# The sums of the retention's block products on VectorE in place of GpSimd

## The chip, the cores and the metric

One core of a Trainium2 chip runs the whole program. The metric is the device time of one launch in microseconds (us); before the change the median of three runs is 1839.34 us, from 1838.33 to 1842.97. Five engines share the work: TensorE (PE), VectorE (DVE), ScalarE (ACT), GpSimd (POOL), and SyncE (SP), which issues loads.

## The reference

Two layers over 512 latent tokens with 256 context tokens in front, 1024 wide, in float32. The first layer is neighbourhood attention beside spatial gating, the second a two-way retention; each is followed by a gated feed-forward with a depthwise convolution. The part that the change touches is the input projection of the retention:

```python
    splits = [RET_QK_WIDTH, 2 * RET_QK_WIDTH, 2 * RET_QK_WIDTH + RET_V_WIDTH]
    q, k, v, g = jnp.split(h_lat @ w_in, splits, axis=-1)
    cos, sin = axial_rope(T, dk)
    q = apply_rope(q.reshape(B, T, H, dk), cos, sin)
    k = apply_rope(k.reshape(B, T, H, dk) * dk ** -0.5, cos, sin)
    ...
    for d in range(2):
        lg = log_decay[d].astype(jnp.float32)
        ...
        s_ctx = retention_final_state(rev(kc), rev(vc), lg)
        outs_lat.append(rev(retention_chunked(rev(q), rev(k), rev(v), lg, s_ctx)))
    y_lat = retention_output(outs_lat[0] + outs_lat[1], g, gn_g, w_out)
```

There are 8 heads; per head q and k are 128 wide, v and g 256.

## The kernel before

Every float32 matrix is split into a high part (ScalarE rounds it, line 225) and a low part (VectorE takes the rounded one from the whole, line 226), and each product is three matmuls of the parts (lines 269 to 272). `split` is the helper for this, and most rows on L225 and L226 in a profile are its two halves.

The retention goes head by head. Head 0 is computed plainly. From head 1 on the projections of a head onto the latent tokens are 2 by 2 block products that need seven block products instead of eight: q beside k (`qk_lat`) and v beside g (`vg_lat`) share them. For that, sums and differences of blocks are needed on both sides:

- of the tokens, once: `token_sums`, whose inner function `whole` (line 1275) puts the high and the low part of a token block together again, 8 times over 128x512;
- of the weights, in each of heads 1 to 7: `q_units` makes four sums of 128x512 in the raw tiles `rwk` and `rwq`, and `vg_units` four of 128x1024 in the raw tiles `rwv0`, `rwv1`, `rwg0`, `rwg1`, all through `less` (line 1293).

Each sum is then split: `rwq` are the split sums for q and k, `rwt` those for v and g. `blk` names token blocks, `w` weight blocks, and `xv`, `yv`, `zv` (`xk`, `yk`, `zk`) the products in PSUM. What else a head does: `rope` on q and k (ScalarE swaps halves into `swk` and `swq`, GpSimd multiplies them by the sine on line 1489, VectorE does the rest on lines 1488 and 1490); `decay` (the tables `e`, GpSimd on lines 1477 and 1478); scores `sd` of keys and queries; states `st` (VectorE on 1549); `across` (VectorE on 1612); `norm` (statistics and lines 1638 and 1646 on VectorE, the power on GpSimd, lines 1632 and 1635, into `rrr`), whose result `rg` is turned by TensorE (`rt`); and the output product `wr`, whose pieces ScalarE copies (`ypr`) and GpSimd adds to DRAM by DMA (`yd`, lines 1463 and 1465). Beside all this runs background work for the modulation of later sub-layers (`acc`, `ac`, `at`).

The order in which each engine takes its instructions is not that of the code. A packed table `ORDER` at the head of the file holds, engine by engine, the place of each instruction, and `queue` chains every engine's instructions in that order.

Of the kernel before, what the change touches and what calls it, by code (L numbers as in the profile page):

```python
# [18 lines left out]
P = 128  # L19
D = 1024  # L20
# [36 lines left out]
70M0x?I?CWMV-2`$;}u~a7)3ymZEOpZ3D<4cx3#Gw{!di1Rgwwmn;=a*ibH8R`>1Qx7G0+<K0d1P6*+CJ8Wm6--f$e5;FX*>RTFeU@NsosNjdz(t2x4Yi
O*s<p7jhra#D*0J_2b4xn?(9)|9%Qa79l19?<)Q!~^6W+z1nMgUT|Y&cYgh~}#_Krt8!_V=~RIOu30fJ__EjZaU(@DMdd<FE2&u`LB}Nuy5z?vw6@N9eA
<;t_Co2IjT_$cNE$>Hff`UIb}eym%R)k%5)vmAzhATNU>01*`7syGO?#0C<7*%HD|6(F#p~w+iH8(B0Jy9RR&O_`r{C{G`DFVRS^I_njS3EIoYV;TwaaH
_%LEr-8xou|61tKD@{<Kwtli-<*RU=)XEVG&~4n;{Zc#7x|3>Izgj5zRdvW7UjPb{)gb;P*mcH`Rfni5JU6jZWyo4diu`KVL#fhb_Z^rrF#K%7${!8(sd  # L60
Y$J$)Z$hwzel3Ru7%{~~*yDV-gs{ww=Bg=6pW<|c{*Xb0G9=#3X%Wus@#o;mx+_~qMdX8rfrK+^*QtLUcBWBdj_z#eZXhn`?Bu$yl%n0Er!sUpl?!iMG>
0WL2!;7vH27ab^~-3pMM1T^vZ*oBK1et}^m*frglT;_lSSD_cZs0+?&u0erZvc9dZt&Rr(7MHl?+>PGN=CU~crA9iM;=tY3O#kxA)2zP_-p5pkAB7Xg;W
m4cO;0@ra0BLM=VoDH{@PW5hi`1G(;2-lv%h73!=E3++gJqnHC8$H_ju1w2xuLEbE^lo@XyYXQt$Rbc!GU}LH>vAmUi||clyXe0JVeAbm8LFYqRiJ{fqN
|$IhQC<S)Xf84eMR<!h|Fas13F7(y$5knPmYkB!f-b`rpe^%!XvrIkk;YvfZHqO=VR4v@!Mr%s-_bIEMZ{W~>1H4XC%aPQzO=OCR4Ay&X5cfE#I+`C-wD
u(xa+1=p1a`_YNb+%Es`YHBFynn>WR}qO1ZXd)*!7eAC!kzYy+5ckD^?mm{_(%4?8IH|Y*nY@m*Wv5zO}6(R8G7pYkD2pZ?8Zp92J7Er_l(Z#3_iv3(Dr
QxzrijZdy37rJu(ZaR<zM?v!+k&9-4gUI*?~g!1QO>33@^=lFym5=Jwgw*|E;PY!5&7B*F$dFmh8%YYXJO@Cv)mk@CXDCt3JotmZa{t>MM9HlU#hX3$g0
# [35 lines left out]
gX1ORLAcU_s%o-Yf&a*Ui*a!JnH$Mn)ciQgs4$+x16$lC-BKi%B18~W`q*~e;!e4EcRIv%JWi5Sm8R(eK4}o;V=SV~IUob2?g&iW!WbF2e{l{E6tE?2nE
-UeD|Mr#$=-LiMYnV=%Os~NRbG8h<qK5YuUFwi!+SBLDX2Hy9mkHsiJKjrylhRBdhx=~vsW3xRZp|qd1bfzxScui8v8hVjfUF`;`iCVCi(hv49WTZR7?9
V6Nf|+r!}O~ud-(N5Sv(ij<puQ!>V^2?%%SeZ!q{a<At*u*VkbmVk*GG{PfiH)aiE^Oq_n3J<X_ExgWm4-exnfzvo>HfeYXl7*#N5k!63%{=yB!KSsRx4
1ZEiQLm;0&y#r+!Q;1D9&i65Lo1OoA(%tfrc!&OfyZDUhR>Zk=~i}*ew+=Fz{IGAI>7Ob+-Q;tCsb>{XQO%m?9Pku$r}PLj1l!tMYErDd(JI7H-cOJl@V
kp%CkAlTI#b9dnuk*+y`O^aNDm^Y-=F!!W^&e(k#HBYjZRjUTm{&MY1Ddc^zOfh#K7R>1lbWPDb@scxeo&Onj7obo)L+fl1rLUtlFF1WK41xpP8PTD<Qt
-94o$=<*tW4<BT_1WV8N5u_7$(sN)Q2rZY6M-J#N)5IpJ+`fu~abRol4Yo<QS9*{m_1lbB<DO+ZwL<=Y0I##mZHDlMNDk}Q^9B6ScAN2<KHolw-Uc)yh;
GnWo7scA$R=mW15U%e!LV^7<}Z_OZbtO1B?1IeJW*{Z_oCfLc))g>9Q61UmK#A!cqMdtOmRrj>{04ie5d$Vuc)Va4i3p}Drrt)AC%b;p{}2NEJ*k=>5z$
# [84 lines left out]
class Trunk:  # L193
# [1033 lines left out]
    def retention(self, y, final):  # L1227
        S, V, T, G, a = self.S, self.V, self.T, self.G, self.a
        KS = float(np.float32(P) ** np.float32(-0.5))
        with ExitStack() as ctx:  # L1230
# [31 lines left out]
            def token_sums():  # L1262
# [1055 lines left out]
```

## Time and profile before

| | us |
|---|---|
| median of three runs | 1839.34 |
| the profiled execution | 1838.39 |
| its span, first to last instruction | 1836.6 |
| TensorE busy | 1754.9 (96%) |
| VectorE busy | 1504.3 (82%) |
| ScalarE busy | 1108.7 (60%) |
| GpSimd busy | 517.6 (28%) |

Busy time is the time in which an engine has an instruction under way; an instruction that is held up while it runs counts as busy. Line numbers are those of the kernel before; in the changed one they are three higher from the table on, as the packed table is three lines longer there.

### The profile page before, as it was taken

How to read it: one execution, taken by the hardware profiler on the slowest of the kernel's cores; microseconds unless marked ns; L12 is line 12 of the kernel's file. 1: busy time of each engine (PE TensorE's matmuls, PEld its weight loads, DVE VectorE, ACT ScalarE, POOL GpSimd, SP SyncE). 2: the span in 40 equal slices, each digit the busy share in tenths (PEclk: the TensorE clock that was granted, in tenths of full speed). 3: DMA queues.
4: the chain of work that ended last, by engine and by line, in shares of the span. 5: the costliest groups of instructions: out<-in, count | busy, mean ns of one | idle time of the engine just before them, and what ended most of it. 6: DMA issues, size and time to landing. Idle time of an engine off the chain costs nothing. (4 is left out here: it accounts for less than half of the span.)

```text
span 1836.6 us, 29516 instructions
## 1 busy us (share of the span) xinstructions
PE 1754.9 (96%) x11108; PEld 1577.7 (86%) x11108; DVE 1504.3 (82%) x2430; ACT 1108.7 (60%) x2029; POOL 517.6 (28%) x574
## 2 busy tenths in 40 slices
PE   8999999999999999999989999889988989999998
PEld 4888888799999998998878888888877889999997
DVE  4887878898788878888898787876867799998887
ACT  7534668775556565556755555554544477676774
POOL 1102222311233222121354454444354110222221
PEclk9999999999999999999999999999998989999999
DMA  8445321454787777878514445444540344887773
GB/s 295 128 143 153 99 84 53 147 154 144 167 191 182 167 167 161 183 165 254 177 47 132 125 134 116 109 109 88 152 93 25 139 139 145 199 218 185 177 170 124
DMA packets 91380, 268.19 MB, mean 146 GB/s; under 512 B 11858, under 2 KB 12370, under 8 KB 91236
## 3 DMA queue, kind: packets, MB, share of 16 engines
q1 hardware_dynamic: 55620, 193.37, 32.7%
q0 software_dynamic: 33312, 64.54, 21.3%
q10 hardware_dynamic: 2304, 8.39, 1.2%
q8 instruction: 87, 1.43, 0.3%
q14 instruction: 57, 0.47, 0.1%
HBM read 193.89 MB, written 52.43 MB: 134 GB/s over the span
## 5 line engine op out<-in xcount | busy, mean ns | idle before, releaser
L380 DVE SCALAR_TENSOR_TENSOR acc<-ar,cs,acc 128x512 f32<-128x512 f32 x256 | 196.4, 787 | 10.2 <-DMA acc<-in_adab_row 4.1
L2006 POOL DMA_DIRECT2D yf<-yp x64 | 56.4, 973 | 260.2 <-ACT yp L2002 231.1
L269 PE MATMUL px<-hs,wc 128*128 128x384 f32 (+1 forms) x480 | 110.0, 309 | 0.2 <-ACT pre L1846 0.2
L269 PE MATMUL px<-blk,wb 128*128 128x384 f32 (+1 forms) x480 | 107.0, 308 | 0.0
L2002 ACT COPY yp<-wf 128x512 f32<-128x512 f32 x118 | 68.7, 584 | 60.5 <-PE wf L272 49.5
L1859 DVE SCALAR_TENSOR_TENSOR cv<-pre,cw,cv 128x769 f32<-128x769 f32 (+1 forms) x88 | 77.5, 884 | 28.9 <-ACT cv L1858 28.8
L1858 ACT ACTIVATE cv<-pre,cw 128x770 f32<-128x770 f32 (+1 forms) x88 | 81.0, 924 | 27.7 <-DVE pre L1851 19.7
L269 PEld LDWEIGHTS px<-hs,wc 128*128 128x128 f32 x480 | 81.3, 188 | 6.4 <-ACT pre L1846 1.0
L1846 ACT ACTIVATE pre<-px 128x256 f32<-128x256 f32 (+2 forms) x160 | 55.6, 369 | 50.7 <-PE px L269 32.7
L269 PEld LDWEIGHTS px<-blk,wb 128*128 128x128 f32 x480 | 80.1, 188 | 6.0 <-ACT pre L1846 1.3
L2006 POOL DMA_DIRECT2D yd<-yp x48 | 45.0, 954 | 142.1 <-ACT yp L2002 137.7
L2006 POOL DMA_DIRECT2D yd<-ypg x48 | 46.8, 1035 | 117.0 <-ACT ypg L2002 116.7
L1862 DVE SCALAR_TENSOR_TENSOR cv<-pre,cw,cv 128x769 f32<-128x769 f32 (+1 forms) x88 | 77.2, 883 | 1.0
L269 PE MATMUL px<-hs,wd 128*128 128x384 f32 x240 | 71.3, 337 | 0.0
L269 PE MATMUL py<-blk,wc 128*128 128x384 f32 x240 | 68.7, 337 | 0.0
L225 ACT ACTIVATE wb<-s 128x512 fp32r<-128x512 f32 x80 | 49.1, 628 | 31.6 <-PE px L269 29.0
L225 ACT ACTIVATE wc<-q 128x512 fp32r<-128x512 f32 x80 | 48.9, 625 | 22.3 <-PE py L269 11.0
L226 DVE TENSOR_TENSOR wb<-s,wb 128x512 fp32r<-128x512 f32 x80 | 54.3, 686 | 9.2 <-ACT wb L225 8.9
L226 DVE TENSOR_TENSOR wc<-q,wc 128x512 fp32r<-128x512 f32 x80 | 54.2, 687 | 4.2 <-ACT wc L225 3.9
L270 PE MATMUL wf<-fo,g 128*128 128x512 f32 x144 | 56.3, 397 | 0.4 <-ACT yp L2002 0.4
L271 PE MATMUL wf<-fo,g 128*128 128x512 f32 x144 | 56.4, 395 | 0.1
L272 PE MATMUL wf<-fo,g 128*128 128x512 f32 x144 | 55.5, 394 | 0.0
(1773 smaller groups left out, 7039.2 us busy)
## 6 DMA issues: line engine op xcount, KB each, us to landing
ar<-in_adaw SPq DMA_DIRECT2D x96, 512.0 KB
yf<-yp POOLq DMA_DIRECT2D x64, 256.0 KB, 5.0
yd<-yp POOLq DMA_DIRECT2D x54, 256.0 KB, 4.8
yd<-ypg POOLq DMA_DIRECT2D x54, 256.0 KB, 5.5
fin<-xd SPq DMA_DIRECT2D x8, 512.0 KB
xn<-in_x SPq DMA_DIRECT2D x6, 512.0 KB
xb<-in_x SPq DMA_DIRECT2D x6, 512.0 KB
xd<-xb ACTq DMA_DIRECT2D x6, 512.0 KB
```

Source lines behind the costliest of these rows:

```text
L225: self.S.activation(hi, src, AF.Copy)
L226: self.V.tensor_tensor(out=lo, in0=src, in1=hi.bitcast(F32), op=ALU.subtract)
L269: mm = lambda *p, **k: self.T.matmul(*p, skip_group_check=True, **k)
L270: mm(out, lhs[0], rhs[0], start=first, stop=False)
L271: mm(out, lhs[0], rhs[1], start=False, stop=False)
L380: V.scalar_tensor_tensor(out=acc[s], in0=raw[:, kk * 512 : kk * 512 + 512], scalar=self.cs[:, 8 * s + k : 8 * s + k + 1], in1=acc[s], op0= ...
L1846: S.activation(pre[:, i, c : c + w], ps[:, b : b + w], AF.Copy, scale=scale)
L1858: S.activation(d, s, AF.Identity, scale=w1, bias=b)
L1859: V.scalar_tensor_tensor(out=d[:, 1:W], in0=s[:, 0 : W - 1], scalar=w0, in1=d[:, 1:W], op0=ALU.mult, op1=ALU.add)
L1862: V.scalar_tensor_tensor(out=d[:, 0 : W - 1], in0=s[:, 1:W], scalar=w2, in1=d[:, 0 : W - 1], op0=ALU.mult, op1=ALU.add)
L2002: S.copy(v, ps)
L2006: G.dma_start((yd[t] if first else y[t])[:, o], v, accum_op=ALU.add)
```

## The change

Two helper functions issue to VectorE (`V`) what they issued to GpSimd (`G`), and the table of orders is another one. The number of instructions of the program is the same; 64 of them, 28 of 128x1024 and 36 of 128x512, change engines.

```diff
@@ ORDER
-c-oD82ecdKb>{sCGlRi241mF)_woR|-g_^6y^@cQkL9sS6sy=oijpWxlqI>yawJ){<w%x`Y{|AP+p*)mPP}olC7Wz=a*{YcC)rKBn@#MT-JDH1C!1{c-h
+c-oD82b3e%b>;h&P^bb5g#u8>IW^Ge1{$4n&S|Enr)PRXhY2Jn4~H|16T~4!QX)lCBu!DGC{lqGgJemhDA|&{mV<1cW39dR@p073I*#ijuhTl5vuk_zy^
...
@@ token_sums
                     def whole(x, n):
                         t = self.t2k(f"f{n}{m}", shape=(P, 2, 256))
-                        G.tensor_tensor(out=t, in0=x[0][:, c].bitcast(F32), in1=x[1][:, c].bitcast(F32), op=ALU.add)
+                        V.tensor_tensor(out=t, in0=x[0][:, c].bitcast(F32), in1=x[1][:, c].bitcast(F32), op=ALU.add)
                         return t
@@ retention
             def less(out, x, y):
-                G.tensor_tensor(out=out, in0=x, in1=y, op=ALU.subtract)
+                V.tensor_tensor(out=out, in0=x, in1=y, op=ALU.subtract)
```

On every engine the order is the same up to the end of the first feed-forward and again from the first blocks of the second one. Between them most instructions move by a few places on their engine. Three places follow. In the rows the trailing numbers are those of buffers, and the digit ahead of them is the head (`rwv05r` is the raw tile rwv0 of head 5).

GpSimd in head 5, around its first sums for v and g, before:

```order
L1293 TENSOR_TENSOR rwv05r_13110<-rwg05r_13112,rwv05r_13110 128x1024
L1477 TENSOR_TENSOR e05_12853<-e05_12853,e15_12855 128x384
L1478 TENSOR_TENSOR e05_12853<-e05_12853,ident_95 128x128
L1465 DMA yd1r_9102<-ypr_13032 128x512
L1489 TENSOR_TENSOR swk5_12973<-swk5_12973,sin_9095 128x512
L1465 DMA yd1r_9102<-ypr_13042 128x512
L1293 TENSOR_TENSOR rwg05r_13112<-rwg15r_13149,rwg05r_13112 128x1024
L1465 DMA yd2r_9103<-ypr_13052 128x512
L1489 TENSOR_TENSOR swq5_12983<-swq5_12983,sin_9095 128x512
```

VectorE at the same place, before:

```order
L226 TENSOR_TENSOR rwv15_13145<-rwv15r_13143,rwv15_13145 128x1024
L1380 TENSOR_TENSOR qs5_12876<-qs5_12876,yk5_12878 128x256
L226 TENSOR_TENSOR rwv05_13114<-rwv05r_13110,rwv05_13114 128x1024
L1488 SCALAR_TENSOR_TENSOR ks5_12875<-ks5_12875,cos_9093 128x512
L226 TENSOR_TENSOR rwt15_13178<-rwv05r_13110,rwt15_13178 128x1024
L1490 TENSOR_TENSOR ks5_12875<-ks5_12875,swk5_12973 128x512
L1488 SCALAR_TENSOR_TENSOR qs5_12876<-qs5_12876,cos_9093 128x512
L226 TENSOR_TENSOR rk15_12972<-ks5_12875,rk05_12971 128x512
L1490 TENSOR_TENSOR qs5_12876<-qs5_12876,swq5_12983 128x512
```

VectorE there, after the change:

```order
L229 TENSOR_TENSOR rwv15_13145<-rwv15r_13143,rwv15_13145 128x1024
L1383 TENSOR_TENSOR qs5_12876<-qs5_12876,yk5_12878 128x256
L229 TENSOR_TENSOR rwv05_13114<-rwv05r_13110,rwv05_13114 128x1024
L1296 TENSOR_TENSOR rwv05r_13110<-rwg05r_13112,rwv05r_13110 128x1024
L1491 SCALAR_TENSOR_TENSOR ks5_12875<-ks5_12875,cos_9093 128x512
L229 TENSOR_TENSOR rwt15_13178<-rwv05r_13110,rwt15_13178 128x1024
L1491 SCALAR_TENSOR_TENSOR qs5_12876<-qs5_12876,cos_9093 128x512
L1493 TENSOR_TENSOR ks5_12875<-ks5_12875,swk5_12973 128x512
L1296 TENSOR_TENSOR rwg05r_13112<-rwg15r_13149,rwg05r_13112 128x1024
L229 TENSOR_TENSOR rk15_12972<-ks5_12875,rk05_12971 128x512
L1526 SCALAR_TENSOR_TENSOR kd15_13086<-kn51_13095,e05_12853,kd05_13085 128x256
L1493 TENSOR_TENSOR qs5_12876<-qs5_12876,swq5_12983 128x512
```

The two sums of `rwv05r` and `rwg05r` stand on VectorE now, the first right behind the split that reads the same tile, the second ahead of the split of k; `rwt15`, the split of the first sum, has one VectorE instruction between itself and the sum, in which ScalarE makes the high part. The two adds of line 1490 (1493 now) still follow GpSimd's products.

GpSimd in the norm of head 6, before:

```order
L1632 TENSOR_SCALAR rrr6_14285<-rmv6_14284 128x2
L1635 TENSOR_TENSOR rrr6_14285<-rrr6_14285,mhalf_107 128x2
L372 DMA acc1100_16118<-in_adab_row 1x16x32
L1293 TENSOR_TENSOR rwv07r_14501<-rwg07r_14503,rwv07r_14501 128x1024
L1477 TENSOR_TENSOR e07_14336<-e07_14336,e17_14338 128x384
L1478 TENSOR_TENSOR e07_14336<-e07_14336,ident_95 128x128
L1293 TENSOR_TENSOR rwg07r_14503<-rwg17r_14540,rwg07r_14503 128x1024
```

GpSimd there, after:

```order
L1635 TENSOR_SCALAR rrr6_14285<-rmv6_14284 128x2
L1638 TENSOR_TENSOR rrr6_14285<-rrr6_14285,mhalf_107 128x2
L1480 TENSOR_TENSOR e07_14336<-e07_14336,e17_14338 128x384
L1481 TENSOR_TENSOR e07_14336<-e07_14336,ident_95 128x128
L375 DMA acc1100_16118<-in_adab_row 1x16x32
L1492 TENSOR_TENSOR swk7_14456<-swk7_14456,sin_9095 128x512
L1492 TENSOR_TENSOR swq7_14466<-swq7_14466,sin_9095 128x512
```

VectorE there, after:

```order
L1641 TENSOR_SCALAR on61_14305<-of6_14204,rmv6_14284,rrr6_14285 128x256
L1632 BN_AGGR rmv6_14284<-rbs63_14295 128x2
L1649 TENSOR_TENSOR rg6_13579<-on61_14305,rg6_13579 128x256
L1641 TENSOR_SCALAR on62_14308<-of6_14204,rmv6_14284,rrr6_14285 128x256
L1641 TENSOR_SCALAR on63_14311<-of6_14204,rmv6_14284,rrr6_14285 128x256
L434 SCALAR_TENSOR_TENSOR ab11_112<-at19_14474,ng_99 128x4
L1649 TENSOR_TENSOR rg6_13579<-on62_14308,rg6_13579 128x256
L1649 TENSOR_TENSOR rg6_13579<-on63_14311,rg6_13579 128x256
L229 TENSOR_TENSOR rwq37_14333<-rwk7r_14199,rwq37_14333 128x512
L1296 TENSOR_TENSOR rwg07r_14503<-rwg17r_14540,rwg07r_14503 128x1024
L1375 TENSOR_TENSOR ks7_14358<-ks7_14358,zk7_14362 128x256
```

Before, two sums and the two steps of `decay` stand on GpSimd right behind the power that `on` waits for. Now the two steps of `decay` alone follow it, and on VectorE the sum of `rwg07r` stands behind the last of the four products `rg`.

VectorE at the end of head 1, around the first sums for q and k of head 2, after:

```order
L1526 SCALAR_TENSOR_TENSOR kd11_10117<-kn11_10126,e11_9873,kd01_10116 128x256
L229 TENSOR_TENSOR rv11_9850<-vs1_10172,rv01_9849 128x512
L1445 TENSOR_TENSOR rg1_9851<-rg1_9851,xv1_10138 128x512
L383 SCALAR_TENSOR_TENSOR acc150_10019<-ar153_10475,cs_93,acc150_10019 128x512
L1592 TENSOR_TENSOR sd11_10343<-rs11_10342,e01_9871 128x256
L1296 TENSOR_TENSOR rwk2r_10479<-rwq2r_10597,rwk2r_10479 128x512
L1592 TENSOR_TENSOR sd11_10343<-rs11_10342,e01_9871 128x256
L1296 TENSOR_TENSOR rwq2r_10597<-rwq2r_10597 128x512
L229 TENSOR_TENSOR rwq12_10601<-rwq2r_10597,rwq12_10601 128x512
```

The first of these sums (`rwk2r`, with the loaded tile `rwq2r`) stands behind the add on `rg1` and a step of `acc`, and half of the scores `sd11` behind it. On SP's queue the loads of the retention exchange places by one to six; the load of `rwq1r` is among those that move back.

More of the change, by code (lines that the diff above doesn't have):

```diff
@@ L57 @@
[L57 to L66, printed above, removed]
@@ L102 @@
[L102 to L106, printed above, removed]
@@ new lines @@
+Y~;8(a0zX2qM6A(+KQ=<^W9z-A>D@+#0#vucd+-PxRbR+|L$Q0(Y6L`SMQWKmT!xK<A2NT#BOhKus1W+tsQ?bDon28NSA3zos7Zy*BjsWCy(`YaJX9w+I
+2?|C0bQn7yr%v6o#?2Usa!bM9)||_Y!v;`55EcB1!#Q#kyyv&^k@;L68%n1N+TPW@`|BTLyt{GU2_ewy5BO8i>xWyf7$o_qc3ufcgI_H-Llgc|&978jtG
+<zH>pB!#C!b}D0G-hI44{3#e-JwN=R4tK0LY_SDlJe3m>HL37y^i=QvqKAg1WP*2sz7V_4c$WIO%91fMgA5;FA+DI6#fj{A;{fY)i!<>GYeI`()#VSGXG
+fidVqlDVRL~Kt7C~OXCAS^}?cgao}TsW(Jm*mRB9HdzY|x70ex9zj1Zs1i*8wTX6*KdKD^wLk03M=<Mi(IzV?9e&Me*ep7#+FgzsF`}R8I@(<kq!2SKh_
+oJD}PJR8OBR$X$J@}A8fS%qdk1-2f(0g%kV6Y!XMgazD=lDPYouIifzbydh7KOhT{!XxQDw-nEx%=+LDTbB{oiJLS5qr+eVn5n0c6uK?MPmVU7|30?r{g
@@ new lines @@
+f>x_Umr4&fs+6tI9j{sw!7sqOXSf5E;<;n;nor9yE4Z2+roSM%9d*zn0yCr|wee)wfJweowcuX3Vq7rN;)7{A`9*|lQ9_b_{oJ@`6<IooR<&%w;y*w9=v
+z=g#k4#HkLXG0F{mW9+fpovFE&YnB_9>YlRmtF4hB@Q@n5xUWfI^dMvFes2q?!0#G-Zkn4SXktiYrN>)Oge@0pKqqCDGnO1-G*mr`7zep15YvyB3p3u2t
+2~Bv&o4o0QbY}%<K%z&t19*@WB0hR_KoI7umnCf9A)_IE)2=Uu8|(|B7RNSU~FloZhv*AAf9a<hu_XgooL?3^ISfuIi_5cBh9d1W-N*m9ytAUYda`J0G0
++pX|)(Y~~z%f#DR<Tz-aiHjkb>4g+ZAXW3@?%*g26u66=AX(vY7BzgIAbD4Y!LzG^9{e9%I=J8|4Z$2`WZv32>oS1~UdANOYmeP<&`VcE%fxBL@if5O0x
+{BfbQFbeM@44_<_8Qxhz4&?dIUGOY<SU582M-*?NWm`09>tUXKV$!kLB}sPK7;?w{+;36yvz1MI<*4dWN)(7|IN@-NB@l3zs2q!>eON7=h<zu^BRNCvkc
@@ new lines @@
+U}&EPlKx$Q^UOzoi=h*!}@zs)M2zj0~o-ur+&YYZmeU`OeIZX}<Rr;G!qUSr$sJ*h5!?J<N6bYSGB)@m!H9q=i3A4kfw=dQEB%dFgJ4qL;Ar~H71BA7u>
+DGcn);Qsa7UFp`l82?`7y(TiGdx~_*R>Lq*4A$c@=(Zsx$IvFf!G4ns-@M)5z!mU!;<vwMUt@d!8b2q9o`zILBT)Yt_OlG_0iiJbBKtD)@P|If9^za|NY
+nm-&V=r`6H$)_eAq_(L!4SU3R~MSW$%NZ^zu^}3=;L?rB*Y)Lm__0gBn1jao6(5T^XNM-i_#JnB_%-BV1+>>`Z7ca!D$Lz3Iz_Lj*w4G|1A)QxPeha)1Q
+oBy{eIb9x|V$+T1~pAQa>jgRFJc8fNmt=8EDY9^~gIcs>(NfQBoS`+XYc`bxQW#6EJY^H&z{*Kuj<E<g=V8;N)tyY8}vTfVW$odZvTXJHBS^z@S8MH()k
+!ydJeV9-3M^P@2Su<PJ*2fvK>&hOuy1j*P2HOw9#uXkbs3QmhIv-{y{ek(piS{~vHA3|?eZTY^gEV>heJ`*l*cqb1mr;qJlfQ)Rg#MKMiZK6g44xH!jGo
@@ new lines @@
+&K9n@y$kMW8O7(Zt4DdA<|t9W7UFWF1N@r2n1vG}*yw^+G0{(B65hs6(##^J!h9AYmr4k3AwYb~<DOkdm6>_4;9XNb6vw7!Zi<b&_B?d`3N&7<X{8@|Kd
+LyhEKT84$TfIsjV_6|!_788|0!}9|BDK<2$LDTfY%4gXGvc+|F1)S>rk1*9a(Afdq7h8Os>N-2ZAxQL-l<1-XL?hAq@3JR_H`%YVLx<sj+jV$p`BByk$B
+q|@TJpCk=%N32*!P&GBP<`->j+=iLb?b6cWHQ=eT*f|iC#AZ)_h3bW-sa?NCkChU09r+nghhJjYk+rU1Pg<T>;zlMhN8l%cvlH=pil({+0b3%k=mCF8+X
+UD3u->9!d|w(*oSN8=Y<Gp8gT|KF$m|Fgl12?fzZ%3vB;A7mmHozQFEWPC>wrAB5-TedLv-Xa=W>`lD=n&~7ajX6;}i*%c1qmuG0WvJ1w?`awm!2y1aug
+JhvtD7r$_31nH6ga63ji$d!^vp;5V@yzfL#kJYu?rGslYpdVe{QK-zIb<0>&EQ18r)6%w?1HXR4;+Mv(o^g>p+;~3HeO{jvsTmKz@e8J3JJ9Kb+)f%wbT
@@ new lines @@
+MD4X^HWA#<Td!zf4I&uwgO0M3?6@NR4xOIu%K2i&l(9MCZ~blA7CfXXk^RLVo=+LNrlmYbiucD2;>Fk7pwV>87<rt4=JJjV9U<%=tOUP6CJ<Rw5CfHCA0
+ly^(e>z+U~!3W}linh^7>ZPlvx3}!dwABEunQ@W2GD$+AYC!R@8)<{$j4N1(td5cnD>s)>Emh%7_7>9;P}>9}0<DKXhmXXLX0lyib6vEYO4qy?Rd-{jQ3
+Tl&htW>4_Il5{iK;A{t4-q*B9QAA>XRnaN=-=mD4$4#eTwawEu>%x2^prQr;2cXabZ7&<!`cvG9av|bdYOJ>YApsj$1wBI87bnFS1WCKWgX8Ut}RebwW$
+sF@!2Sk&2Q!w}Vq>a-QHxWc`3mDa=&0r4ogSUKcci(OsL*;SiALVXdEFGtv%Re4@2?-IMa-(@{x-zhfR|TH>HeT(9_GqB9yvfSD|HWHa4XCX1NsP<nc8^
+ygS-%u#EOfo{8zvtwGR$s#EqbSCh_-kwQKgL0hcga|v4gtdLoqJJ$l#3*T8_!j#%Q{Khk&xX`&2-7sfGqVM+GS8u<SDB=x{V;LZWum3CV^9rF^!s!9>kM
@@ new lines @@
+{xVjL>=)^-{yr6waCb|k=6f(r*-F6f>?{LSTkD6LUC8nJjROy1oNH9z%y*1jpQQ{Dap2NTeXp9(8*;A<=-C7URKuYQFkjH{nyb4P8(K%jn`U5NlH(Kpx^
++0@4KtnR9|E}<W9W&<HP<*E+!m(itAiEmtqMS33`*JHkZpwuqx291az+=CN<vzQ#f$seE;<=Aly8><ssJV6P9ziSb^h@KDz#PGp^c`y~O?mb2>->T=;Ts
+3g^V8EY<M$%1lz0kEUexbMLQpSd^OBXMtRyH$z{Rnp})jX_?VwTXnMjW?J;w_PE<g~5TE{GHd8bqvjL>svSz}6n{rqTvjWbZtfc)ECKYBL?Q69^~ciTcz
+-l#@zw8CrzX7zoHCv!(OfwyV3TWOz<bPi<!g2HoMZ1A4ZRm}mO?=1mn%h7t->mU^DXLCFn73Q$r`!lgnQg^#Wk+{m=wVLyj~5Q`hGfdjwAX8KSL?>@BK^
+2k;e-EsfCfg!m9v%MtV(T~GJX-5sv+sez&vFF)BYWe*0%)ftG*A{44`GIg=jkIa{M86WT`!lFmkWI81Os*&u3I`}F+R1u)59wO5Fg2)aoo9=Ir9dZUT)F
@@ new lines @@
+yPBnIrCP-o$cL`kwL$~csrR0dszN*MA^g+oIgK@H=h^?gb6f<TD?{~SG$%08L{$&CMX{*97|B>E9Mkt5v#ZC#<fk4_?c1x><9qCC2kPTEv83^zol=D{fy
+KDd86{()b4ha6lOfDi3YqtXotc1|=_dNF~NWYgW)F3F2GYU2VgiYnkUK|)60%EssCPoyFPcu==fz|dO52e)C~-UX^gA)qy=m=rNd>f4nxrHs;!hPpYAG*
+*Qe4fqDkTT&ZsuaAs!El#FDX(Q17co+TW2&D0$e~9-_7ZiuA!OnZkDX^!4-spIvd10pt<xp;|#nYeY^FKP!8uLzi$w~Lz=$OzjdgD#wm&UR--2CO%LH9K
+-#Rr%>Wv_T5uDVrIO-IDI(1bybqL6l~Ad99YOF^FWfG)ad4tQZtabsMY(9l1qD;#RWt~hJj&FY!NDVCU-dP0e|(3pDKF@u&<9Ar%1C6Y!epYB^0xZPa*#
+-H%nZ3R4XZJZzMCBXjySL-VQ
```

205 lines of the change are left out of this document (94 added, 111 removed).

## The prediction

> **What bounds the kernel now.** First I read the busy time by stretch of the span. The columns are the stretch and its length in us, then the busy us (and instructions) of TensorE (PE), its weight loads (PEld), VectorE (DVE), ScalarE (ACT) and GpSimd (POOL), the granted TensorE clock, the DMA share and GB/s.
>
> ```profile
> 0.00:800.00 800.00, 790.08 (x4479) 689.37 (x4480) 644.36 (x1134) 490.26 (x953) 186.23 (x264) 1.00 0.60 154
> 930.00:1480.00 550.00, 489.47 (x3430) 450.69 (x3428) 431.11 (x635) 292.24 (x479) 230.71 (x190) 0.96 0.42 112
> 1480.00:1600.00 120.00, 118.70 (x856) 111.53 (x856) 114.58 (x182) 88.01 (x163) 14.82 (x17) 0.97 0.55 153
> ```
>
> TensorE is the bound, and outside the retention there is little to win: it is idle for 10 of the first 800 us and for 1.3 of the 120 behind it. The retention, 930 to 1480, is the exception: 60.5 us idle (550 less 489.47) and a clock of 0.96, which is another 22 us (0.04 times 550). The instructions that the change moves, and nearly all that it puts in another order, are there too. Next I asked what TensorE waits for in that stretch: the waiting instruction, what released it, us in total, times, the longest.
>
> ```profile
> PE rt L1659 <- DVE rg L1646: 6.7, 4, 4.7
> PE xv L269 <- DVE rwt L226: 5.9, 4, 1.9
> PE yv L271 <- DVE rwt L226: 5.8, 3, 3.9
> PE rx L270 <- ACT st L225: 5.7, 5, 2.1
> PE zk L270 <- DVE of L1612: 3.8, 1, 3.8
> PE ac L418 <- ACT ah L225: 3.6, 1, 3.6
> PE pf L270 <- ACT hb L225: 3.4, 1, 3.4
> PE rs L272 <- DVE rk L226: 3.3, 1, 3.3
> PE ac L418 <- DVE al L226: 2.7, 1, 2.7
> PE kn L1519 <- DVE ks L1490: 2.6, 1, 2.6
> PE rs L270 <- ACT rq L225: 2.5, 1, 2.5
> PE rs L271 <- DVE rq L226: 1.5, 1, 1.5
> ```
>
> Mostly it waits for VectorE, which is busy for only 431 of the 550 us. So VectorE is late without being full. The timeline around the 3.9 us wait shows how (start, duration, instruction): first GpSimd, then VectorE, then TensorE.
>
> ```profile
> 1261.85 1.61 POOL L1489 TENSOR_TENSOR swk<-swk,sin 128x512 f32<-128x512 f32 x1
> 1263.69 2.99 POOL L1293 TENSOR_TENSOR rwg05r<-rwg15r,rwg05r 128x1024 f32<-128x1024 f32 x1
> ...
> 1261.94 5.83 DVE L226 TENSOR_TENSOR rwt<-rwv05r,rwt 128x1024 fp32r<-128x1024 f32 x1 [0.65 <-ACT rwt L225]
> ...
> 1267.83 0.39 PE L271 MATMUL yv<-rwt,s1r 128*128 128x256 f32 x1 [3.93 <-DVE rwt L226]
> ```
>
> One VectorE instruction took 5.83 us, and it ended 1.1 us after the second of two GpSimd instructions that had run since it began. The same shape elsewhere takes 1.22 us, as the rows for the feed-forward below show. So the two engines exclude each other while both read two tensors of SBUF, and the sums of lines 1275 and 1293 are most of what GpSimd does with tensors here.
>
> **The change, part by part.** Rows: GpSimd's time on lines 1293 and 1275; VectorE's free durations, in the second feed-forward (wa, 128x1024, and wc, 128x512); then the groups that are stretched in the retention.
>
> ```profile
> 930.00:1480.00 550.00, 118.88 (x56) 0.96 0.42 112
> 930.00:1480.00 550.00, 12.18 (x8) 0.96 0.42 112
> ...
> 1500.00:1740.00 240.00, 19.53 (x16) 1.00 0.70 176
> L226 DVE TENSOR_TENSOR wc<-q,wc 128x512 fp32r<-128x512 f32 x40 | 27.3, 687 | 2.1 <-ACT wc L225 2.1
> ...
> 930.00:1480.00 550.00, 55.77 (x28) 0.96 0.42 112
> L226 DVE TENSOR_TENSOR sd<-sd,sd 128x512 fp32r<-128x512 f32 x16 | 18.9, 1178 | 0.2 <-ACT sd L225 0.2
> L1490 DVE TENSOR_TENSOR qs<-qs,swq 128x512 f32<-128x512 f32 x7 | 9.8, 1394 | 5.5 <-POOL swq L1489 5.3
> L1490 DVE TENSOR_TENSOR ks<-ks,swk 128x512 f32<-128x512 f32 x7 | 9.2, 1313 | 2.7 <-POOL swk L1489 2.7
> L1488 DVE SCALAR_TENSOR_TENSOR qs<-qs,cos 128x512 f32<-128x512 f32 x7 | 9.2, 1310 | 0.9 <-ACT swq L1483 0.9
> L1488 DVE SCALAR_TENSOR_TENSOR ks<-ks,cos 128x512 f32<-128x512 f32 x7 | 5.1, 725 | 9.2 <-ACT swk L1483 9.2
> L226 DVE TENSOR_TENSOR rk<-ks,rk 128x512 fp32r<-128x512 f32 x7 | 7.8, 1114 | 4.9 <-ACT rk L225 4.8
> L226 DVE TENSOR_TENSOR rq<-qs,rq 128x512 fp32r<-128x512 f32 x7 | 7.4, 1056 | 0.0
> ```
>
> Off GpSimd: 64 instructions, 118.9 + 12.2 = 131 us. By itself this is worth nothing, as GpSimd is busy for 231 of 550 us. The transfers that GpSimd issues (the yd pieces) stay on its queue, behind fewer instructions. On SP's queue loads change places by one to six; in the stretch only two waits of a sum for a load show, those of the second rival below, and with them I price this.
>
> Onto VectorE: 28 sums of 128x1024 at 19.53/16 = 1.22 us are 34.2 us; 28 and 8 of 128x512 at 0.687 us are 24.7 us. Together 58.9 us.
>
> Back to VectorE: the time for which GpSimd held it up. The 28 rwt instructions (55.77 us) would take 34.2 free, so 21.6. sd: 16 times (1178 less 687) is 7.9. rk 3.0 and rq 2.6. The two groups of L1490: 7 times 707 and 7 times 626 ns, 9.3. L1488 on qs, against the 725 ns of the same instruction on ks: 7 times 585, 4.1. That makes 48 us. The last 13 (L1490, L1488) stand beside the products swk and swq, which stay on GpSimd, so between 35 and 48 come back; I take the middle, 42.
>
> So VectorE does about 17 us more in the stretch, 448 in place of 431. Is that on the path? In 1480 to 1600 it is busy for 114.58 of 120 us with TensorE at 118.70, so a share of 0.95 holds nothing up there; 448 us in some 510 is 0.88. The cover is VectorE's idle time, 119 us now. I charge the 17 us at the rate at which its work now makes TensorE wait (the rows above name VectorE for 32 us, over 431 busy), 1.3, and call it 2. If that cover is gone, the cost is the whole 17, or 24 with the lower figure.
>
> What TensorE gets: the waits whose releaser is one of the stretched groups or hangs on one: 6.7 (its rg stood behind locked instructions), 5.9, 5.8, 3.3, 2.7, 2.6, 2.5, 1.5, together 31.0 us. Not all of that is the moved sums' doing (swk has 1.6 of the 4.6 us in the timeline); against it I leave out zk and the ac behind ScalarE, 3.8 and 3.6 us, which come out of the same queues. I count no gain for the waits on st, which no stretched row explains. The new order of all engines inside the retention I cost at nothing of its own: it shifts most instructions by a few places, it is what has to place 64 new VectorE instructions where nobody waits, and no row prices that; its bounds are the rivals below.
>
> The clock follows the idle time. TensorE is idle in 1264 to 1268 and gets half its clock right afterwards:
>
> ```profile
> 1264.00:1268.00 4.00, 0.17 (x1) 0.17 (x2) 4.00 (x2) 0.00 (x0) 2.69 (x2) 1.00 0.71 96
> 1269.00:1272.00 3.00, 3.00 (x14) 2.71 (x12) 0.69 (x1) 0.63 (x2) 0.37 (x1) 0.50 0.00 0
> ```
>
> With 31.0 of 60.5 us of idling gone I take the same share of the 22 us: 11.3. [...]
>
> Sum: 31.0 + 11.3 - 2 = 40 us. The profiled execution took 1838.39 us (1836.6 of span and 1.8 around it), so 1798; the median of the three runs stands 0.95 above it, so 1799. The ends: nothing gained and VectorE's 24 us all on the path, 1863; all idling and the whole clock loss gone, 82 us, 1757. I stand nearer the middle because the waits that I count have rows of stretched instructions ahead of them.
>
> **The rivals.** First, a wash: VectorE only swaps time under the exclusion for work of its own. For it speaks that at several of TensorE's waits VectorE has been busy throughout, and that 58.9 us come for 35 to 48. What would be left is the shorter way through a sum: half of the 11.7 us of waits on rwt, 5.9, less 2: 1835. Against it: the 5.83 and 4.7 us are single stalls that work in pieces of 1.2 us doesn't make. [...]
>
> Second, slower: VectorE's queue stalls on a load. The first sum of each head's query and key weights needs loaded tiles, and in two heads GpSimd has waited for a load ahead of it:
>
> ```profile
> POOL rwk2r L1293 <- DMA rwq2r<-in_ret_qk: 8.3, 1, 8.3
> POOL rwk3r L1293 <- DMA rwo20r<-in_ret_out: 7.3, 1, 7.3
> ```
>
> On GpSimd nobody stood behind it; on VectorE the splits of scores and values do, and TensorE behind them. Two heads at these prices take 15.6 us of my 40. It decides from six heads on: seven times 7.8 is 55, less 40 is 15 slower, 1854. Against it: in five of the seven heads no such wait shows, and the new order puts the sum of head 2 behind the instruction that VectorE was at when the load had landed.
>
> Third, larger: with no 3 to 6 us stalls the new order closes most of the other waits as well, 55 to 82 us, about 1772. For it: the rest of the program runs with TensorE idle for 1%. Against it: st, hb and the handing over from head to head have no row that ties them to GpSimd.
>
> **How the numbers follow.** Forecast, 15 to 55 us faster, 1784 to 1824: 0.63. Wash, 1824 to 1844: 0.13. Slower: 0.11. Larger: 0.13. A measurement of this kernel can tell about 0.3%, 5.5 us. Faster than that are the forecast, the larger gain and half of the wash, 0.82; within it 0.07; slower 0.11. The range 1772 to 1834 leaves out half of the larger case and nearly all that lies above: about 0.2.
>
> **What would show it.** In the profile after: the sums on VectorE at 1.22 and 0.69 us; rwt near 34 us for 28 (38 with what swk and e still hold); GpSimd at about 95 us in the stretch; VectorE still about 448; no TensorE wait on rwt, rg or rk over 2 us; TensorE idle for about 30 us and the clock at 0.98. The prediction is wrong if waits of VectorE on loads appear ahead of the new sums, if sums stand right before instructions that TensorE waits for, or if swk, swq and e stretch VectorE as much as all of GpSimd does now.

## The result and the profile after

The changed kernel takes 1781.37 us (median of 4 runs, 1779.55 to 1782.02), the kernel before 1838.9 us in the runs beside it: 57.5 us less, a ratio of 0.9681 (95% interval 0.9664 to 0.9698). The profiled execution took 1781.4 us, with a span of 1779.6.

The whole difference lies in the retention. It ends 57 us earlier, so the stretch that answers to 930 to 1480 is 930 to 1423. The table by stretch (columns as in the prediction), with a window of the whole span for each kernel, the changed one first:

```profile
930.00:1423.00 493.00, 472.32 (x3414) 439.00 (x3412) 417.47 (x695) 291.37 (x475) 102.41 (x126) 0.99 0.46 120
1423.00:1783.00 360.00, 345.16 (x2416) 320.54 (x2416) 318.83 (x499) 242.57 (x441) 69.65 (x82) 0.98 0.63 166
0.00:1840.00 1840.00, 1736.87 (x11108) 1568.10 (x11108) 1492.42 (x2494) 1110.48 (x2029) 386.08 (x510) 0.99 0.55 146
```

```profile
0.00:1840.00 1840.00, 1754.93 (x11108) 1577.67 (x11108) 1504.33 (x2430) 1108.71 (x2029) 517.63 (x574) 0.99 0.55 146
```

TensorE is idle for 20.7 us of the stretch (493 less 472.32), before 60.5: 39.8 us. Its busy time falls by 17.2 us (489.47 to 472.32). Together these are the 57. Of the 17.2 us the clock explains 15.1: by the records of the granted clock, which the rounded 0.96 and 0.99 only approximate, half clock costs 5.1 us in this stretch, before 20.2. The surprise is in the VectorE column: 64 more instructions, and less time, 1492.42 us over the program in place of 1504.33.

What TensorE still waits for between 930 and 1423 (waiting instruction, releaser, us in total, times, longest):

```profile
PE rt L1662 <- DVE rg L1649: 4.3, 4, 2.1
PE rx L273 <- ACT st L228: 3.4, 3, 1.6
PE pf L273 <- ACT hb L228: 3.0, 1, 3.0
PE ac L421 <- ACT ah L228: 2.5, 1, 2.5
PE yk L274 <- DVE s1r L229: 1.7, 1, 1.7
PE kn L1522 <- DVE ks L1493: 0.8, 1, 0.8
```

The waits on `rwt`, `rk`, `rq` and `al` are gone. The same stretch for the tile `rwt` alone (busy us of TensorE, its weight loads, VectorE and ScalarE), and then two sums of the changed kernel, a wide and a narrow one, from the views of a tile and of a line (minimum, median and maximum in ns, first and last start):

```profile
930.00:1423.00 493.00, 112.56 (x672) 95.91 (x672) 33.93 (x28) 29.58 (x28) 0.99 0.46 120
```

```profile
L1296 DVE TENSOR_TENSOR rwv05r<-rwg05r,rwv05r x1: 1224/1224/1224, 1228.5 to 1228.5; 128x1024 f32<-128x1024 f32 x1
L1296 DVE TENSOR_TENSOR rwq1r<-rwq1r x1: 685/685/685, 933.4 to 933.4; 128x512 f32<-128x512 f32 x1
```

`rwt` takes 33.93 us where it took 55.77, so 1.21 us for each of the 28, its free time. Nothing holds it up any more.

### The profile page after: what moved, and what is told of

Its sections match the earlier page's. It is cut to its first block, busy times and chain, and to the rows that moved or that the text cites. A ratio compares the mean times of both kernels' runs of the same rounds, so it can differ in the third digit from the quotient of the medians.

```text
span 1779.6 us, 29484 instructions
## 1 busy us (share of the span) xinstructions
PE 1736.9 (98%) x11108; PEld 1568.1 (88%) x11108; DVE 1492.4 (84%) x2494; ACT 1110.5 (62%) x2029; POOL 386.1 (22%) x510
## 3 DMA queue, kind: packets, MB, share of 16 engines
q0 software_dynamic: 33312, 64.54, 21.9%
## 4 chain that ended last, share of the span: by engine, by line
PE 84%; DVE 6%; ACT 4%; issue 3%; POOL 2%; DMA 1%; SPq 0%; POOLq 0%; DVEq 0%; ACTq 0%
PE px L272 12%; PE wf L273 5%; PE wf L274 5%; PE wf L275 5%; PE xv L272 4%; PE py L272 4%; PE px L274 2%; PE px L273 2%; PE px L275 2%; PE yv L272 2%; PE xk L272 2%; PE py L273 1%; PE py L274 1%; PE py L275 1%; PE ug L274 1%
## 5 line engine op out<-in xcount | busy, mean ns | idle before, releaser
L383 DVE SCALAR_TENSOR_TENSOR acc<-ar,cs,acc 128x512 f32<-128x512 f32 x256 | 189.7, 760 | 7.2 <-issue 2.6
L1861 ACT ACTIVATE cv<-pre,cw 128x770 f32<-128x770 f32 (+1 forms) x88 | 81.1, 925 | 27.8 <-DVE pre L1854 20.0
L273 PE MATMUL wf<-fo,g 128*128 128x512 f32 x144 | 56.2, 397 | 0.1
L1635 POOL TENSOR_SCALAR rrr<-rmv 128x2 f32<-128x2 f32 x16 | 5.7, 358 | 232.0 <-DVE rmv L1632 232.0
L275 PE MATMUL wf<-fo,g 128*128 128x512 f32 x144 | 56.0, 394 | 0.0
```

The lines of the kernel that those rows point to most:

```text
L273: mm(out, lhs[0], rhs[0], start=first, stop=False)
L275: mm(out, lhs[1], rhs[0], start=False, stop=last)
L383: V.scalar_tensor_tensor(out=acc[s], in0=raw[:, kk * 512 : kk * 512 + 512], scalar=self.cs[:, 8 * s + k : 8 * s + k + 1], in1=acc[s], op0= ...
L1861: S.activation(d, s, AF.Identity, scale=w1, bias=b)
```

## The experiments

Three theories were open. *Exclusion*: the time came back because GpSimd no longer holds VectorE up. *Order*: it came from the refitted orders. *Short path*: a sum takes 1.2 in place of 2.7 us, and TensorE feels only that.

The table sums up all runs. "Against before" is the median less that of the kernel before in the same comparison (1836.45 to 1839.67 us in these), and in this form the changed kernel stands at -57.5. "Stretched" is worked out from the trace: for each VectorE instruction that starts in 930 to 1480, its time above the fast end (the 5th percentile) of its operation and shape in the same trace, where that is over 60 ns, summed. "Half clock" is what TensorE's stretches at half clock cost over the whole span, the last of them counted to its end. GpSimd's busy time is that of 930 to 1480.

| kernel | us | against before | ratio, 95% interval | stretched us | GpSimd us | half clock us |
|---|---|---|---|---|---|---|
| before | 1838.9 | 0 | 1 | 77.2 | 230.7 | 27.1 |
| changed | 1781.37 | -57.5 | 0.9664 to 0.9698 | 13.1 | 107.7 | 11.8 |
| move alone | 1804.08 | -35.6 | 0.9791 to 0.9824 | 14.6 | 116.2 | 14.5 |
| order alone | 1828.16 | -11.5 | 0.9926 to 0.9955 | 63.7 | 225.9 | 27.8 |
| changed, idle products | 1834.38 | -5.3 | 0.9960 to 0.9993 | 63.4 | 234.4 | 28.7 |
| changed, idle memsets | 1789.04 | -50.6 | 0.9713 to 0.9742 | 11.0 | 215.2 | 15.0 |
| changed, idle copies | 1841.73 | +4.9 | 1.0015 to 1.0034 | 54.4 | 320.4 | 27.7 |
| changed, narrow sums on GpSimd | 1788.16 | -48.7 | 0.9717 to 0.9746 | 30.3 | 157.1 | 9.9 |
| changed, wide sums on GpSimd | 1818.92 | -17.5 | 0.9889 to 0.9920 | 45.2 | 173.1 | 20.9 |
| changed, 92 products on VectorE | 1819.54 | -17.3 | 0.9889 to 0.9918 | 18.5 | 108.0 | 20.2 |
| changed, 28 products on VectorE | 1788.22 | -48.2 | 0.9724 to 0.9750 | 16.7 | 109.7 | 12.1 |
| changed, rope products moved too | 1779.64 | -57.2 | 0.9673 to 0.9706 | 6.8 | 88.4 | 9.8 |
| changed, norm's product on ScalarE | 1783.64 | -52.8 | 0.9697 to 0.9724 | 12.0 | 108.4 | 11.6 |
| changed, old order of loads | 1791.42 | -45.9 | 0.9738 to 0.9770 | 13.5 | 108.9 | 16.6 |

**The move and the order, each alone.** The first kernel has the two lines of the change and the old table, with the 64 sums put into VectorE's row; the second has the lines as before and the new table, with the sums put into GpSimd's row.

```diff
@@ move alone, against the kernel before
-                G.tensor_tensor(out=out, in0=x, in1=y, op=ALU.subtract)
+                V.tensor_tensor(out=out, in0=x, in1=y, op=ALU.subtract)
...
@@ order alone, against the changed kernel
-                V.tensor_tensor(out=out, in0=x, in1=y, op=ALU.subtract)
+                G.tensor_tensor(out=out, in0=x, in1=y, op=ALU.subtract)
```

> The 64 sums run on VectorE, and every other instruction of all engines keeps the order it had before; each sum stands in VectorE's queue where it started on GpSimd in the profile before (the 8 token sums three places later). Exclusion theory (the time came from GpSimd no longer holding VectorE up): most of the 57.5 us is there, 1785 to 1805 us, and VectorE's stretched time in the retention falls from 77 us to under 20. Order theory (the time came from the refitted orders): 1825 us or more. Short-path theory (a sum takes 1.2 in place of 2.7 us, and that alone is what TensorE feels): also near 1800, so this run parts the order from the other two only.

> The sums stay on GpSimd, and all engines take the new order; each sum stands in GpSimd's queue where it started on VectorE in the profile after. Exclusion theory: the same 131 us of GpSimd work stretch VectorE by some 60 to 80 us again, 1830 to 1850 us. Order theory: 1780 to 1800 us. Short-path theory: 1830 to 1850 us.

The move alone gives 35.6 us, the order alone 11.5, both 57.5. So the order theory falls as the main cause, and exclusion and short path stand (1828.16 us is 2 us under the range that these two gave for the order alone); but the order is worth 11.5 us by itself and 21.9 on top of the move, more than either of these theories had given it. The stretch of the move alone, and VectorE's time on `rwt` in it:

```profile
930.00:1446.00 516.00, 477.47 (x3414) 440.58 (x3414) 419.41 (x696) 290.96 (x477) 111.22 (x126) 0.99 0.44 119
930.00:1446.00 516.00, 35.58 (x28) 0.99 0.44 119
```

`rwt` is free already (35.58 us), and the half clock down to 14.5 us, but TensorE is idle for 38.5 us (516 less 477.47). Its longest wait is one of 4.2 us for VectorE; none of the others is over 3.4:

```profile
PE rx L268 <- ACT st L223: 4.7, 5, 1.3
PE zk L268 <- DVE of L1610: 4.2, 1, 4.2
PE pf L268 <- ACT hb L223: 3.4, 1, 3.4
PE rt L1657 <- DVE rg L1644: 3.2, 3, 2.0
PE stl L269 <- DVE rv L224: 2.8, 3, 1.4
```

The new order takes another 17.8 us of idle time away (38.5 to 20.7). It does so in head after head: from the first transposes of a head's output (`rt`) to those of the next, from head 1 to head 7, the move alone takes 68.3, 68.6, 66.4, 64.9, 68.3 and 60.2 us, the changed kernel 64.5, 64.3, 64.9, 62.6, 65.5 and 54.5. The first transposes, those of head 0, come 5.6 us earlier (949.9 against 955.5 us), and only from there to head 1 the changed kernel takes longer (71.1 against 68.0).

**Work on GpSimd that nobody waits for.** These two part exclusion from short path. The changed kernel gets idle instructions at the places of the sums, into a scratch tile of its own.

```diff
@@ idle products
+        self.scr = self.cp.tile([P, 384], F32, name="scr", tag="scr")
...
             def less(out, x, y):
                 V.tensor_tensor(out=out, in0=x, in1=y, op=ALU.subtract)
+                for _ in range(out.shape[-1] // 512):
+                    G.tensor_tensor(out=self.scr, in0=cos[:, 0:384], in1=sin[:, 0:384], op=ALU.mult)
@@ idle memsets
+                for _ in range(3 * (out.shape[-1] // 512)):
+                    G.memset(self.scr, 0.0)
```

> The changed kernel, with GpSimd given work of the old kind that nobody waits for: at each sum's place it multiplies 128x384 of the two rope tables into a scratch tile, once for a sum of 512 columns and twice for one of 1024, 92 products of about 1.3 us, 120 us in all. Exclusion theory: VectorE is stretched by some 55 to 70 us in the retention again while it also does the sums, so 1820 to 1850 us. Short-path and order theories: nothing waits for these products, 1780 to 1787 us.

> As the kernel with the idle products, but each product replaced by three memsets of the same 128x384 scratch tile, 276 of about 0.4 us: about the same GpSimd time, which reads no tensor. Exclusion theory (only GpSimd instructions that read SBUF beside VectorE exclude it): 1779 to 1788 us and VectorE's stretched time stays near 13 us. If a busy GpSimd as such holds things up (its queue, its DMA issues): 1800 us or more.

The idle products take nearly all of the gain back, 52.2 of 57.5 us, with nobody waiting for them but twice, for 0.3 us each; the memsets, of about the same busy time on GpSimd, 6.9. VectorE's time on the 28 `rwt`, with the products and then with the memsets:

```profile
930.00:1480.00 550.00, 43.63 (x28) 0.96 0.41 108
```

```profile
930.00:1480.00 550.00, 33.97 (x28) 0.98 0.44 119
```

So the exclusion, 52.2 less the 6.9 of the memsets, is shown to be worth some 45 us in the new order. The short path cannot be the cause: with the shorter sums and the new order both in place, 5.3 us of the gain are left once the exclusion is back. The 6.9 us of the memsets, 1 us more than the exclusion theory allowed, come without stretched time. They fit a busy GpSimd as such: TensorE's `kn` waits 2.7 us for `ks`, whose product `swk` stands in GpSimd's queue, where the changed kernel has 0.8 (VectorE's longest wait for `swk` is 3.1 us, in the changed kernel 1.2), and the half clock costs 3.2 us more.

A third one asks what GpSimd must do to exclude VectorE: three copies in place of a product, one tensor read in place of two.

```diff
@@ idle copies
+                for _ in range(3 * (out.shape[-1] // 512)):
+                    G.tensor_copy(out=self.scr, in_=cos[:, 0:384])
```

> As the kernel with the idle products, but each product replaced by three copies of 128x384 from a rope table to the scratch tile, 276 of some 0.45 us: GpSimd reads one tensor and not two. Parts two readings of the exclusion: if it takes two inputs on both engines, the time is as with memsets, 1785 to 1793 us; if any GpSimd instruction that reads SBUF holds VectorE's two-input instructions up, 1815 to 1840 us.

One tensor read is enough. The copies stretch VectorE by 41.3 us more than the changed kernel has (54.4 less 13.1), and are stretched themselves, from 0.49 us at the fastest to 0.85 in the mean, so that GpSimd is busy for 320 us and its own products come late too (one add on `ks` stands 4.24 us for `swk`, where the longest such wait in the changed kernel is 1.2); the row of the copies:

```profile
L1298 POOL COPY scr<-cos 128x384 f32<-128x384 f32 x252 | 214.2, 850 | 13.8
```

The products read two tensors, the copies one and the memsets none: beside them VectorE's stretched time is 63.4, 54.4 and 11.0 us.

**Which sums did the harm.** In the changed kernel one size of sums goes back to GpSimd; the eight token sums go with the narrow ones. The diff is that of the first of the two kernels.

```diff
             def less(out, x, y):
-                V.tensor_tensor(out=out, in0=x, in1=y, op=ALU.subtract)
+                E = V if out.shape[-1] == 1024 else G
+                E.tensor_tensor(out=out, in0=x, in1=y, op=ALU.subtract)
```

> Half the move: the 28 sums of 128x1024 on VectorE, the 36 of 128x512 (54 of the 131 us of GpSimd) left on GpSimd, in the new order. Exclusion theory: 54/131 of the 64 us of stretched time comes back, 26 us, and 54/131 of what the idle products cost, 22 us: 1795 to 1812 us. If only the wide sums did harm: 1779 to 1787 us. If the narrow ones did most: 1815 us or more.

> The other half of the move: the 36 sums of 128x512 on VectorE, the 28 of 128x1024 (77 of the 131 us of GpSimd) on GpSimd, in the new order. The narrow half gave back 17 us of stretched time and 9 us of the gain. If the rest of the 64 us belongs to the wide sums, VectorE is stretched by some 45 us more than in the changed kernel, and the kernel loses 30 to 45 us of its gain: 1811 to 1826 us. If the exclusion's cost is about even per us of GpSimd, 12 to 15 us: 1793 to 1797 us.

The narrow sums, 54 us of GpSimd, cost 8.8 us, less than an even share, and between the two ranges of their forecast; the wide ones, 77 us, cost 40.0. The two add up to 48.8, about what all sums cost in the new order (46.0 from the order alone). The wide ones put TensorE's waits on `rwt` back:

```profile
PE xv L268 <- DVE rwt L225: 9.0, 6, 2.8
PE rt L1659 <- DVE rg L1646: 7.9, 3, 3.9
PE yv L270 <- DVE rwt L225: 3.9, 2, 2.0
```

Per us of stretched time the wide sums cost 1.25 us (40.0 over 32.1), the narrow 0.51 (8.8 over 17.2). That the longer single stalls make this difference fits the 5.83 us of the prediction, beside a rope product of 1.61 and a wide sum of 2.99 us; it was not tested by itself.

**The price of VectorE's time.** The prediction charged 17 us of it at 2. Here the idle product stands on VectorE, behind all sums (twice behind a wide one) or behind the wide ones alone, as in the diff.

```diff
             def less(out, x, y):
                 V.tensor_tensor(out=out, in0=x, in1=y, op=ALU.subtract)
+                if out.shape[-1] == 1024:
+                    V.tensor_tensor(out=self.scr, in0=cos[:, 0:384], in1=sin[:, 0:384], op=ALU.mult)
```

> The changed kernel with idle work on VectorE in place of GpSimd: behind each sum one product of 128x384 into a scratch tile (two behind a wide sum), 92 of 0.55 us, 51 us in all, that nobody waits for. This prices VectorE's time in the retention, which the prediction charged at 2 us for 17. At that rate 6 us: 1783 to 1793 us. If VectorE's cover is used up and each us of its work ends on the path: about 1830 us. Exclusion theory: VectorE's stretched time stays near 13 us, whatever the time.

> The changed kernel with the idle product of 128x384 on VectorE behind the 28 wide sums alone: 28 times 0.55, 15.5 us, nearly the 17 us that the prediction charged at 2. By that rate 1782 to 1784 us. By the price that the 92 products showed (40 us for 51), 1792 to 1795 us. If VectorE has some cover that the larger load used up, in between or below, 1781 to 1788 us.

15.5 us of work cost 9.3 us, 51 us cost 40.2: 0.6 and 0.8 us for each. These are prices per us of free duration; GpSimd's remaining products stretch some of the idle products too, which take 18.3 and 57.5 us in the traces, and by that time the prices are 0.5 and 0.7. The intervals are some 3 us wide to either side, so the two rates are not clearly different. There is little cover, although VectorE is idle for 75.5 of 493 us (493 less 417.47). Both kernels add the work at one kind of place, between a sum and its split. With the small load, `xv` waits for `rwt` again, six times and never for more than 0.8 us:

```profile
PE xv L269 <- DVE rwt L226: 3.0, 6, 0.8
```

**Going further.** Two kernels follow from these prices: the rope products leave GpSimd too, or VectorE is relieved at ScalarE's cost.

```diff
@@ rope products moved too
-                G.tensor_tensor(out=sw, in0=sw, in1=sin, op=ALU.mult)
+                V.tensor_tensor(out=sw, in0=sw, in1=sin, op=ALU.mult)
@@ norm's product on ScalarE
-                    V.tensor_scalar(
+                    V.scalar_tensor_tensor(
                         out=on,
                         in0=d["o"][:, t],
-                        scalar1=mv[:, t, 0:1],
-                        scalar2=rr[:, 1, t : t + 1],
+                        scalar=mv[:, t, 0:1],
+                        in1=d["g"][:, t, :],
                         op0=ALU.subtract,
                         op1=ALU.mult,
                     )
-                    V.tensor_tensor(out=d["g"][:, t, :], in0=on, in1=d["g"][:, t, :], op=ALU.mult)
+                    S.activation(d["g"][:, t, :], on, AF.Copy, scale=rr[:, 1, t : t + 1])
```

> The changed kernel, and in addition the 16 rope products swk and swq made by VectorE, each in VectorE's queue where it started on GpSimd. Exclusion theory: of the last 13 us of stretched time the 9 beside these products go, for 16 times 0.69, 11 us of work; the chain behind ks and qs gets about 1 us shorter in each head: 1772 to 1781 us. If what is left of stretched time is hidden: 1779 to 1785 us.

> The changed kernel with VectorE relieved: in the norm of each head VectorE makes (of - mean) times the gate in one instruction, and ScalarE multiplies by the reciprocal deviation, where VectorE made two instructions before. VectorE has 32 instructions of 0.42 us less, and 32 that take 0.48 in place of 0.42, 11 us in all; ScalarE 32 of about 0.4 us more. By the price of the 92 idle products (0.75 us for each us of VectorE) 8 us come back: 1770 to 1777 us. If ScalarE, which now waits for both at that place, holds the splits behind it up: 1781 to 1792 us.

With the rope products on VectorE the stretched time falls to 6.8 us, and the time does not move (-57.2 against -57.5): 6.3 us back for 11 of work is a wash at these prices. Relieving VectorE of 11 us does not pay either: 52.8 in place of 57.5 us, at the edge of the two intervals. TensorE's wait for `rg` has moved from VectorE to ScalarE, and grown from 4.3 to 7.1 us:

```profile
PE rt L1658 <- ACT rg L1645: 7.1, 7, 2.6
ACT rg L1645 <- POOL rrr L1631: 6.3, 1, 6.3
```

ScalarE keeps to the order of the table and stands at the new ones for their inputs: once, in the last head, 6.3 us for GpSimd's `rrr`, and four times for VectorE's `on`, 5.6 us in total. The sums were worth moving for the exclusion that they caused, not for the engine's load. None of these beats the changed kernel.

**Which part of the order.** The changed kernel with the old order of the loads on SP's queue. The orders of TensorE, VectorE and ScalarE depend on each other, and were not tried apart.

```diff
@@ one place of SP's queue, where 51 of 404 places change
+DMA rwv11r<-in_ret_vg 128x1024
...
 DMA rwo00r<-in_ret_out 128x1024
 DMA rwo01r<-in_ret_out 128x1024
-DMA rwv11r<-in_ret_vg 128x1024
```

> The changed kernel with SP's queue of loads in the order that it had before (51 of its 404 places differ); TensorE, VectorE, ScalarE and GpSimd keep the new order. It tells which part of the new order makes the 22 us that the changed kernel has over the move alone. If it is the order of TensorE, VectorE and ScalarE: 1779 to 1784 us. If it is that of the loads: 1795 to 1806 us.

Neither of the two: 11.6 us are lost, and one place has them all. ScalarE waits for a tile of head 0's output weights, and TensorE behind it; the load of that tile is issued at 962.6 us, in the changed kernel at 913.1. The waits of this kernel, with that of SP's own queue, and its timeline on SP:

```profile
ACT rwo L224 <- DMA rwo00r<-in_ret_out: 10.4, 1, 10.4
PE xk L268 <- ACT ks L1369: 10.3, 1, 10.3
SPq L210 <- DVE rwq L225: 50.2, 2, 49.3
```

```profile
961.72 0.33 SPq L210 DMA_DIRECT2D rwv11r<-in_ret_vg  x1
962.10 0.43 SPq L210 DMA_DIRECT2D ar<-in_adaw  x1
962.57 0.43 SPq L210 DMA_DIRECT2D rwo00r<-in_ret_out  x1
```

SP keeps to its order too: the load of `rwv11r` waits 49.3 us for VectorE to free its raw buffer, and `rwo00r`, now behind it, is issued 0.85 us after it; the new order has it ahead. From head 1's transposes on the heads take what they take in the changed kernel (64.7, 64.3, 64.8, 62.6, 64.5 and 54.5 us from `rt` to `rt`). So the order's gain in the heads is that of the compute engines, and the order of loads has to fit it at one point.

## Why the prediction was right, and where it was off

The direction and the mechanism were right, but for one detail: the prediction has the two engines exclude each other while both read two tensors, and the copies show that one tensor read on GpSimd's side is enough (54.4 us of stretched time against 13.1); how many VectorE has to read was not tried. 1781.37 lies in the range, in the part of it that belongs to the third rival. The size was not that of the likeliest case: I said 40 us, it was 57.5, and the likeliest case ended at 1784. By its time this is that rival, which said that without the long stalls the new order closes most of the other waits as well; the kernels with the move and the order alone show that this is what happened. Step by step:

- *Off GpSimd, 131 us*: 131.5 (517.63 less 386.08). Worth little by itself: the idle memsets put back 107.5 us of GpSimd's time and cost 6.9, where the prediction had nothing.
- *Onto VectorE, 58.9 us*: 60.7, namely 36.1 for the 28 wide sums and 24.6 for the 36 narrow ones.
- *Back to VectorE, 35 to 48 us*: mis-sized. VectorE is busy for 11.9 us less with 60.7 us more to do, so 72.6 came back. Of these 5.3 are only overlap: a VectorE instruction often begins some 0.08 us before the last one ends, and such overlaps add up to 154.8 us after the change, 149.5 before. The instructions themselves got 67.3 us shorter. The groups that I had listed gave 42, my middle: 21.8 from `rwt`, 7.9 from `sd`, the rest from the others, with the 2.8 us taken off by which L1488 on `ks` got longer. What I had left out are groups whose single instructions lose little but which are many, such as the sums of the modulation (`acc`) and the normalization (`on`). VectorE's time on these two tiles, `acc` first, before the change and then after it:

```profile
930.00:1480.00 550.00, 35.85 (x40) 0.96 0.42 112
930.00:1480.00 550.00, 18.80 (x32) 0.96 0.42 112
```

```profile
930.00:1423.00 493.00, 30.23 (x40) 0.99 0.46 120
930.00:1423.00 493.00, 12.72 (x32) 0.99 0.46 120
```

- *VectorE's net 17 us, charged at 2*: both halves were wrong, and by luck they hid each other. The net was 13.6 less in the stretch (431.11 to 417.47), not 17 more; and the rate was 0.6 to 0.8 us per us, not 0.12. Had 17 us been added, they would have cost about 10 at that rate. The idle 119 us were little cover; why, no run shows.
- *TensorE's waits, 31.0 us*: of the rows that I had counted 5.1 us are left (`rt` 4.3, `kn` 0.8), so 25.9 went. With the move alone 9.6 of the 31.0 us are left, so 21.4 went, nearly all of the 22.0 us of idle time that it saves. In the changed kernel another 13.9 us went from waits that I had not counted. Of these 6.5 are the `zk` and `ac` that I had set against the rest (3.8 to 0.7, 3.6 to 2.5), and `rx` on `st` (5.7 to 3.4), which I had said no stretched row explains; the others are short.
- *The clock, 11.3 us*: 15.1 in the stretch. It came with the idle time, of which 39.8 and not 31.0 us went; the share that I took would have given 14.5 with the right idle time.
- *The new order, nothing of its own*: this is the term that was mis-sized most. It is worth 11.5 us alone and 21.9 on top of the move. Against the move alone, 35.6 us, my sum of 40 was close, in part by the luck of VectorE's term. Why the order is worth more once the exclusion is gone was not tried; that it then closes short waits which the stalls of 3 to 6 us had covered is my guess.
- *The rivals*: no wash. On loads the new sums wait twice, 2.1 and 1.0 us, so the second rival did not come; but its mechanism is real, as ScalarE's 10.4 us with the old order of loads show, from a single load.

Of the signs that I had named, the sums' durations, `rwt`, and GpSimd's time hold (102.4 us in the stretch, forecast 95). TensorE's idle time (20.7, forecast 30), the clock (0.99, forecast 0.98) and VectorE's (417, forecast 448) are better than named. `rt` still waits for `rg`, four times and for up to 2.1 us.

## What to carry to other kernels

Before counting what work costs on the engine that gets it, count what it costs the neighbour now: compare each VectorE group with its free duration, small groups included, since here they held 25 of 67 us. Here VectorE, busy for 85% of the stretch and feeding the bound, had little free time: price what is added to such an engine at 0.6 to 0.8 us per us until a run says otherwise. Moving 11 us of it to ScalarE, in the norm, gave nothing back. When an order is fitted anew together with a change, give the order a term of its own; here it was 22 of 57 us.

## What the runs showed of the hardware

In these traces the half clock comes in fixed periods. In all 14 the stretches at half clock begin on one grid per trace, of 3.41 us (within 0.01 us, 3 to 12 of them in each), and last one, two, three or five of its periods, but for the last, which the end of the program cuts. A wait of 3.41 us is not needed for it: in the changed kernel the wait of 2.5 us for `ah` lies for 1.9 us in one period, and the next one is at half clock:

```profile
1327.90:1331.30 3.40, 1.51 (x13) 1.30 (x11) 3.07 (x5) 2.04 (x5) 0.00 (x0) 1.00 0.03 5
1331.30:1334.70 3.40, 2.79 (x11) 2.50 (x12) 2.38 (x6) 2.75 (x6) 0.00 (x0) 0.50 0.00 0
```

Over all traces, of 6575 periods at full clock that begin between 100 and 1770 us with TensorE idle for less than 35%, none is followed by a half one; of 60 with 35 to 50%, 3; of 45 with 50 to 60%, 28; of 50 with more, all. Of 10 periods at half clock with 20 to 35% idle, 9 are followed by another one. So in the changed kernel a wait with 1.9 us in one period was followed by 3.4 us at half clock. With the narrow sums on GpSimd the same wait for `ah`, 2.5 us too but cut by the grid, cost no clock (half clock costs 9.9 us over its whole span, 11.8 in the changed kernel). Beyond these counts the traces do not show what the clock is granted by.
